# A quarter of the r projection for twelve head pairs, computed in fp32 inside the recurrence

## The chip, the cores and the metric

The kernel runs on one core of one Trainium2 chip. The metric is the device time of one execution in microseconds (us); the times of before are those of three runs, and the rows of the trace come from a fourth, profiled one. PE is the matrix engine (TensorE), PEld its weight loads, DVE the vector engine (VectorE), ACT ScalarE, POOL GpSimd, SP the engine that issues nearly all DMAs; "SPq" in a row is SP's queue.

## What is computed

One inference step of a two-layer decoder: an RWKV-7 layer and an RG-LRU layer, each followed by a causal ConvFFN, for a prompt of 256 rows and a group of 8 sample rows (T = 264 columns, model width 2048 = 16 tiles of 128). The change lies in the RWKV layer:

```python
xx = x_prev - x
xr, xw, xk = x + xx * mix[0], x + xx * mix[1], x + xx * mix[2]
...
r = xr @ w_r
k = xk @ w_k
v = xv @ w_v
...
def _wkv_step(S, inp):
    r_t, d_t, k_t, v_t, a_t, b_t = inp
    sa = jnp.einsum('bhvk,bhk->bhv', S, a_t)
    S = S * d_t[:, :, None, :] + sa[..., None] * b_t[:, :, None, :] + v_t[..., None] * k_t[:, :, None, :]
    y = jnp.einsum('bhvk,bhk->bhv', S, r_t)
    return S, y
```

r, k and v are 2048 wide, that is 16 pairs of heads of 64; the scan `_wkv_step` runs over time for every head. All values are float32.

## The kernel before

Values stand transposed: a tile has 128 channels in its partitions and 264 columns (256 prompt, 8 sample). `U0` first holds x, then the mixer's input h, and from the end of the projections on r.

**Projections** (loop over `PARTS` and `projs`, L820 to L858). The 16 input tiles are taken in five parts, the last being tiles 12 to 15; for each part the projections k, v and r follow each other, each in four groups `g` of four output tiles. A matmul of the projections is done in three passes (`mm_pieces`, L446): weights and inputs are split into a rounded high part (`wh`, `ah`) and the rest (`wl`, `al`) of type fp32r, and high x high, high x low and low x high are added in PSUM. Weights come as a stream `ws` of pieces (1024 columns, half of a raw tile of 1 MB), loaded by SP (L419) and split by ACT and DVE (L433, L434) two pieces ahead. Partial sums of parts 0 to 3 stay in `acck`, `accv`, `accr`; after the last part `last_k`, `last_v` send k and v to DRAM (`Kd`, `Vd`), and `last_r` (L800) writes `accr` + PSUM into `U0`. Ahead of the last r projection stands `lora()` (L803 to L816), which makes `lw` from three further mixes of h; its matmuls are plain fp32, with weights not split. With part 12 to 15, the r projection's four groups of two pieces are the last work of this stage.

**Recurrence** (`wkv_begin` to `wk.close()`). Every pair j of heads goes through jobs, written as generators: load, prep, diag, solve, levels, prepb, seq, out; beside them run the sample group (sprep, sixteen pieces `sample`, sgate, send) and 44 "pump" steps, which compute the modulation vectors for later layers from raw tiles of 1 MB (`wm`, L344; loads L1400). A step is what stands between two `yield`s. The order of all steps is a table written out, `ORDER`: a letter names the job, a number in front says how many steps, the number behind is the pair (`3p0`: three steps of prep for pair 0). Every engine then works through its instructions in that order. Prep starts with lora weights `lu` and the row `kj` of k from `Kd`; PE (L972, L974) and ACT make `sa`, DVE `kk`, the scan `cum`, products `b` and `AR` (which needs r, in `U0`); PE multiplies `b` x `AR` (L898); `ma` is copied out, goes through DRAM (`scr`, L1064) to `mb` (L1069) for the solve on DVE (pairs 0 and 1) or POOL, comes back as `xc` (L1096) to the levels, which make `E`, and the scan (seq) uses it, four chunks a pair. The copy `yh` (L1195) is the first step of out, after a pair's scan. Raw tiles in this stage have three buffers (`raw_tile`), shared by pumps and the sample group's weights (`lups`, L1246). After the last pair the out projection begins with pieces of `ws` again.

```python
        for h in range(2):
            SP.dma_start(raw[:, 1024 * h:1024 * h + 1024], I["wmr"][i][:, 1024 * h:1024 * h + 1024])
            yield
```

Of the kernel before, what the change touches and what calls it, by code (L numbers as in the profile page):

```python
# [38 lines left out]
p2 b1 p2 b0 2w1 b0 3p2 4p1 g0 b0 l3 l4 d1 p3 p2 l4 d0 b0 p2 2p3 2b1 w2 3b0 u0 w2 2p3 2p2 2p3 p4 p3 5p2 3p3 2p4
a0 d0 g0 d1 p4 2g0 b2 p2 u1 3b1 2s0 p3 h0 p3 2g0 d2 2l5 2p3 u2 d3 b1 p5 2w3 s0 d2 g0 s0 4g0 w4 g0 2s0 d3 2p4  # L40
2b1 2p3 b1 2p4 4b2 s2 p4 l6 p4 p3 2g0 2p4 w5 2p5 s2 4p5 3g0 4p4 b3 2p4 g0 2p5 u3 3p5 2g0 3b2 b3 p5 2b3 s0 p5
g0 p5 b3 2p5 v0 3p6 2v0 w4 2v0 u4 l6 v1 q0 g0 p6 s2 2g0 a0 l7 p4 v0 p5 w6 v1 p5 s2 3a0 2s2 l7 2p6 a0 p6 2q0
3p7 b2 2v1 w5 u5 2p7 b2 2p6 w6 u6 v0 p6 p7 2p6 2v1 2v0 2b3 2v0 4a0 b3 3h0 2b3 l8 b4 4p7 l8 h0 s2 p8 p7 s4 d5
2p8 h0 2q0 v1 d4 p8 q0 p9 v1 q0 l9 w7 s2 v2 3p7 4h0 2q0 3v1 q0 d4 3q0 l9 2q0 2p9 a1 p7 d5 2q0 p7 s6 p7 p9 6p6
2p7 2q0 a1 2q0 b5 3v2 2q0 d7 2o0 l10 w8 b4 p6 v3 b4 q1 p8 l11 2v2 2q1 w8 q1 v3 2s4 3p8 2v2 v3 a1 w7 s4 q1 2p8
v2 u7 o0 2s4 q1 v3 3q1 v2 q1 d6 2p8 q1 p9 w10 a0 v2 v3 o0 v3 a1 2w9 w10 2a1 2p9 3q1 s4 q1 3a1 2p8 l10 2q1 d6
d7 3o0 s6 q1 o0 a1 u8 u9 2p10 p9 p8 2o0 2p10 3a2 u10 2b4 2a2 b4 a1 3q1 s4 v4 v3 b4 2v3 3a2 2q1 v5 p9 3v4 2v3
2p8 3b5 2b4 2b5 p8 2p9 a2 p9 w12 2o0 v4 b5 b4 2w11 w12 b5 u11 u12 v4 s6 2b5 o0 2o1 l11 6q2 v4 q0 2w13 u13 o0
2v4 2a2 p8 s6 2v5 o1 3a3 2w15 2v4 w14 p9 v5 3q2 2p9 2q2 a3 2p9 a3 d8 p9 2s6 3q2 p10 p11 q2 w14 2o1 2p11 p10
2q2 p9 q2 2v5 2p10 w16 2a3 3q2 o1 s10 d8 q2 s6 2a3 p11 q2 o2 2o1 u14 u15 o1 o2 p10 w16 2p10 q3 p10 v5 3q3 o2  # L50
u16 2v5 a4 v5 p12 o1 v5 s6 v6 b6 2o2 q1 v6 d9 2q3 p11 a3 q3 2a4 b6 a3 p10 3q3 l12 v6 w17 a4 q2 2a4 v6 b6 q3 a4
2b6 3q3 w17 4p10 a4 o1 b6 q3 v6 2b6 p10 l12 3q3 v6 q3 p11 s8 q3 b6 2q3 o3 2a4 o3 a5 q3 a5 w18 p10 w18 b6 2p12
2o2 u17 b7 o2 l13 3q4 b7 p11 3p12 d9 2q4 w19 u18 b7 w19 d10 2o2 5p11 2w20 l13 a5 4q4 2v6 3v7 p12 v7 v6 a5 o2
q4 a4 2s8 p12 2p11 v6 o1 2q4 u19 v6 p12 2o1 o2 s8 2w21 d11 2q4 2p11 a6 3q4 2v7 2p11 w22 p11 q4 w22 3q4 p13 3a5
p13 2o2 p13 2q4 u20 2l14 2p13 u21 o3 p13 o3 2p12 o4 v7 2p12 o4 o3 q5 a5 o4 p14 2a5 2s8 v7 a6 2v7 2w23 q3 s8
2p12 4q5 p13 v7 p12 p14 p12 w24 3a6 o3 a6 2p14 a6 w24 3q5 o4 u22 u23 2q5 2o3 q5 2o3 s8 3o4 2q5 b8 3q5 v8 o3
2b7 2o4 b7 q5 o4 q5 v8 2p12 2b7 a6 q5 2v8 a5 2b8 q5 b8 a6 o3 q5 d10 q4 l15 2p13 3b8 2b7 2v8 2q5 u24 d11 s10
3b8 2w25 2o5 v8 q6 2w26 2s10 2q6 a6 2a7 v8 u25 v8 2q6 v9 2p14 p13 2v8 a7 3q6 2a7 o4 b9 2o3 q6 a7 2b9 a7 3q6
2w27 2o4 l15 u26 o4 p13 u27 s10 3o5 p15 2b9 3p13 w28 q6 w28 w29 2q6 s10 3p13 w29 a7 3q6 a6 b9 s10 q6 q5 q6 2b9
q6 p14 3v9 2q6 3p15 b9 2o5 w30 u28 2p13 b9 3o6 u29 q7 v9 b10 q7 2o5 w30 p14 o5 s14 v9 b10 2a7 b10 3p14 d12 3q7  # L60
3v9 o6 s12 u30 v9 a8 p14 p15 s10 2q7 v9 2q7 p15 o6 p14 p15 q7 2b10 2a8 w31 v10 w31 3q7 2p14 q7 d13 b10 2q7 v10
2a8 2q7 u31 2w32 q7 p14 2v10 b10 2q7 3a8 2p15 a7 q7 2o7 q7 a8 q8 p14 2v10 q6 u32 4q8 v10 2o5 v11 q8 v10 2o5
2v10 d12 d13 s12 2w33 q7 v10 q8 p15 a8 p15 2q8 b11 p15 5b11 q8 o6 a8 b11 2o7 3q8 3a9 q8 u33 3o6 2w34 q8 p14 o7
3q8 o6 w35 a9 o6 w35 p15 2q8 2p15 q8 s12 w36 2p15 s12 a9 o7 2s12 2q8 2o7 2o8 q9 s12 2o6 w36 d14 2q9 a10 2q9 o7
2q9 u34 a9 w37 o6 p15 u35 3q9 d15 2o7 v11 w37 s12 2a9 d14 d15 o8 o7 2a9 p14 2v11 4q9 w38 q9 2o8 a10 q9 u36 q9
a10 4q9 2v11 q9 w38 2o9 q8 q10 p15 2o7 o9 o8 o9 3q10 2o8 a9 2a10 v12 b10 q9 u37 a10 o9 q10 3o9 3o8 2b10 b11
2o9 v12 o9 b12 2q10 2b12 o9 2b11 v12 u38 3q10 s14 2a10 s14 v12 2b12 3q10 s14 q10 q9 v12 b13 2a10 2a11 b13 2q10
2b13 3b12 v12 b13 5q10 o8 w40 o8 o9 5a11 o9 o8 2b12 2q10 o10 a10 3b14 o10 b14 w40 b14 2b13 q11 2o10 2a11 o10
2v11 2q11 2a11 o10 2s14 a12 2v11 4o10 s14 2w39 2b13 v13 b13 v11 2q11 2b14 q10 2q11 s14 3v13 2v12 2q11 w43 2a12
q11 3a12 b14 2v13 3v12 q11 o10 a13 a12 b15 a12 3q11 u39 u40 2a12 3q11 2b14 2q11 2a13 2v13 3q11 o11 a12 a14 b15  # L70
2a13 o11 q12 q11 b15 v13 q11 v13 4q12 3a13 v13 q12 v15 v14 2b15 q12 3o11 2q12 o10 2v14 o11 q12 2a13 b15 o11
3q12 2b15 w42 a14 2q12 3o11 q12 a13 2v14 a15 4q12 o11 a14 q12 v14 b15 q12 b15 2o12 q13 o11 q12 2o10 4q13 2o12
o11 3a14 4o12 v15 4q13 o12 2v15 o11 2a14 o12 q13 o12 q12 2q13 2o12 3q13 2a14 o12 2q13 2v14 a15 4q13 2a15 v14
# [1723 lines left out]
```

## Time and profile before

| | us |
|---|---|
| median of 3 runs (2865.06 to 2867.12) | 2866.76 |
| the profiled execution | 2867.66 |
| its span, first to last instruction | 2865.9 |
| end of the last r projection, from the span's start | 398.0 |
| first matmul of the out projection | 728.06 |

The profiled execution is 0.9 us over the median. Projections take the first 398 us, the recurrence 330 us, and the other layers the rest. In the rows below a time is a start in us from the span's start and the number behind it a duration; `[... <-x]` is how long the engine had been idle and what ended that. "x4" are four instructions in a row: an fp32 matmul is two of them, a matmul of the split kind is one. PEclk is the share of full clock that was granted to PE: 1.00 is 2.4 GHz, 0.50 is 1.2 GHz, and what lies between is a mean of both.

### The profile page before, as it was taken

To read this page: it belongs to the slowest core of one execution; us is meant where nothing else is said; L and a number is where in the kernel's file an instruction comes from. 1 tells how busy PE (TensorE), PEld (TensorE's weight loads), DVE (VectorE), ACT (ScalarE), POOL (GpSimd) and SP (SyncE) were. 2 spreads that over 40 slices of the span, in tenths; PEclk is the share of its full clock that TensorE was granted. 3 is DMA by queue.
4 is the path that set the end of the run, shared out by engine and by line. 5 is a ranking of instruction groups with operands and counts; after the bars stand their busy time and mean duration, and the time that the engine had idled before them with its cause. 6 is when DMAs were issued, how large, how long until landed. Compare 5 with 4: busy or idle time off the path is not lost.

```text
span 2865.9 us, 61683 instructions
## 1 busy us (share of the span) xinstructions
...
## 2 busy tenths in 40 slices
...
GB/s 329 291 259 242 209 121 237 254 263 155 278 247 225 240 249 254 257 247 237 251 254 250 253 241 192 265 228 246 249 228 250 206 179 184 181 177 179 183 187 75
DMA packets 146134, 648.48 MB, mean 226 GB/s; under 512 B 41104, under 2 KB 60704, under 8 KB 77248
## 3 DMA queue, kind: packets, MB, share of 16 engines
...
## 4 chain that ended last, share of the span: by engine, by line
PE 83%; DVE 6%; ACT 3%; DMA 3%; issue 2%; POOL 1%; SPq 0%; DVEq 0%; POOLq 0%; ACTq 0%
PE bk L454 18%; PE bk L455 17%; PE bk L456 17%; PE sq L454 7%; PE sq L455 7%; PE sq L456 7%; PE wm L344 5%; DVE wl L434 1%; PE bk L898 1%; DMA raw<-in_wmr 1%; ACT wh L433 1%; DMA rawx<-in_wst 1%; DVE bt L548 1%; PE sq L812 1%; POOL xs L1087 1%
## 5 line engine op out<-in xcount | busy, mean ns | idle before, releaser
L434 DVE TENSOR_TENSOR wl<-raw,wh 128x1024 fp32r<-128x1024 f32 x448 | 552.3, 1235 | 498.6 <-ACT wh L433 489.5
L433 ACT CAST wh<-raw 128x1024 fp32r<-128x1024 f32 x448 | 468.6, 1048 | 643.6 <-PE bk L455 430.0
L454 PE MATMUL bk<-AH,wh 128*128 128x264 f32 x2352 | 670.6, 285 | 0.9 <-ACT wh L433 0.9
L456 PE MATMUL bk<-AH,wl 128*128 128x264 f32 x2352 | 669.1, 284 | 1.7 <-DVE wl L434 1.5
L455 PE MATMUL bk<-AL,wh 128*128 128x264 f32 x2352 | 668.7, 284 | 0.8 <-DVE AL L492 0.8
L434 DVE TENSOR_TENSOR wl<-rawx,wh 128x1024 fp32r<-128x1024 f32 x312 | 381.6, 1225 | 331.7 <-ACT wh L433 326.6
L433 ACT CAST wh<-rawx 128x1024 fp32r<-128x1024 f32 x312 | 326.5, 1048 | 457.8 <-PE bk L455 337.4
L454 PE MATMUL bk<-ah,wh 128*128 128x264 f32 x1822 | 524.8, 289 | 9.8 <-ACT ah L491 5.5
L456 PE MATMUL bk<-ah,wl 128*128 128x264 f32 x1822 | 520.9, 286 | 0.4 <-DVE wl L434 0.4
L455 PE MATMUL bk<-al,wh 128*128 128x264 f32 x1822 | 521.2, 286 | 0.0
L454 PEld LDWEIGHTS bk<-AH,wh 128*128 128x128 f32 x2352 | 443.3, 188 | 20.2 <-ACT cv L1537 8.4
L456 PEld LDWEIGHTS bk<-AH,wl 128*128 128x128 f32 x2352 | 441.7, 188 | 2.7 <-DVE wl L434 2.7
L455 PEld LDWEIGHTS bk<-AL,wh 128*128 128x128 f32 x2352 | 442.6, 188 | 1.0 <-DVE AL L492 1.0
L454 PEld LDWEIGHTS bk<-ah,wh 128*128 128x128 f32 x1822 | 344.1, 189 | 28.1 <-ACT wh L433 8.7
L456 PEld LDWEIGHTS bk<-ah,wl 128*128 128x128 f32 x1822 | 344.8, 189 | 1.5 <-DVE wl L434 0.8
L455 PEld LDWEIGHTS bk<-al,wh 128*128 128x128 f32 x1822 | 345.0, 189 | 0.7 <-DVE al L492 0.2
L454 PE MATMUL sq<-AH,wh 128*128 128x264 f32 x1040 | 296.7, 285 | 0.1
L455 PE MATMUL sq<-AL,wh 128*128 128x264 f32 x1040 | 295.6, 284 | 0.0
L456 PE MATMUL sq<-AH,wl 128*128 128x264 f32 x1040 | 295.4, 284 | 0.0
L1530 POOL COPY fgs<-gt 128x10 f32<-128x10 f32 x88 | 53.2, 632 | 1307.7 <-ACT gt L1524 1286.7
L454 PEld LDWEIGHTS sq<-AH,wh 128*128 128x128 f32 x1040 | 196.0, 188 | 9.6 <-ACT cv L1537 4.2
L455 PEld LDWEIGHTS sq<-AL,wh 128*128 128x128 f32 x1040 | 195.7, 188 | 0.0
(462 smaller groups left out, 4490.2 us busy)
## 6 DMA issues: line engine op xcount, KB each, us to landing
...
```

The lines of the kernel that those rows point to most:

```text
L344: PE.matmul(ps[32 * g:32 * g + 32, :cols], cs[:, k0 + kk, :], raw[:, (kk * 4 + g) * cols:(kk * 4 + g + 1) * cols], start=(k0 + kk == 0), s ...
L433: S.copy(wh, t)
L434: V.tensor_sub(wl, t, wh.bitcast(F32))
L454: PE.matmul(ps[:, :n], h[:, kk, sl], xh, start=first and kk == 0, stop=False)
L455: PE.matmul(ps[:, :n], h[:, kk, sl], xl, start=False, stop=False)
L456: PE.matmul(ps[:, :n], l[:, kk, sl], xh, start=False, stop=last and kk == 1)
L548: e.tensor_tensor(t, U1[:, j:j + n, :TP], r1[:, None, :TP].to_broadcast([128, n, TP]), op=mult)
L812: PE.matmul(pl[m][:, :T], pc[:, j % 2, m * 128:m * 128 + 128], xm, start=(j == 0), stop=(j == 15))
L898: PE.matmul(out[HH[(i + turn) % 2]], lhs[HH[i]], rhs[HH[i]], start=start, stop=stop, skip_group_check=True)
L1087: E.tensor_tensor(xs[:, s + 1:, :m], xs[:, s + 1:, :m], tv, op=add)
L1530: G.tensor_copy(gs[:, m], gt[:, TP:])
```

## The change

The last r projection (part 12 to 15) keeps group 0 only, so `last_r` runs for the tiles of pairs 0 to 3. For the other twelve pairs POOL copies `accr`, the sum of parts 0 to 3, into `U0`, after lora has read `U0` for the last time. The four mixes of tiles 12 to 15 for r are kept whole in a new tile `mr`. In the recurrence a new job `rest` (letter x) for i = 0, 1, 2 loads the raw tile of two pieces of w_r, multiplies in plain fp32 (four output tiles, four input tiles each, 264 columns: 16 matmuls), and DVE adds each result into `U0`. The stream `ws` ends six pieces earlier in the projections and is set to its old place after the recurrence. `ORDER` is new as a whole.

```diff
-p0 p1 2g0 2l0 2p0 l1 p1 p0 s0 l1 p0 g0 3p0 l2 4p0 p1 l3 2p0 2w0 5p1 2p0 4p1 p2 3p0 p2 2g0 p3 p2 l2 p2 3p1 3b0
...
+s0 g0 p0 l0 2p0 p1 3x0 2l1 l0 p1 g0 5p0 g0 p1 p0 3x0 5p1 p0 w0 p0 l2 2p1 x0 p0 3x0 3p0 2p1 2p0 p2 b0 2p2 2l3
...
+    mr = vres([128, 4, T], F32, "mr")
...
-    ws.limit = P1
+    ws.limit = P1 - 6
...
     def mix_of(j, m, xx):
-        t = a1p([128, T], F32, "mx", 4)
+        t = mr[:, j - 12] if m == 0 and j >= 12 else a1p([128, T], F32, "mx", 4)
...
                 lora()
+                with tc.manual_schedule(engines={mybir.EngineType.Pool}):
+                    G.tensor_copy(U0[:, 4:, 1:], accr[:, 4:])
...
-            for g in range(4):
+            for g in range(1 if b == 16 and w == 2 else 4):
...
+    def rest_of_r(i):
+
+        raw = raw_tile()
+        for h in range(2):
+            SP.dma_start(raw[:, 1024 * h:1024 * h + 1024], I["wst"][(P1 - 6) // 2 + i][:, 1024 * h:1024 * h + 1024])
+            yield
+        w = raw.rearrange("p (a k m) -> p a k m", a=2, k=2)
+        for m in range(4):
+            ps = bank()
+            for k in range(4):
+                PE.matmul(ps[:, :T], w[:, k // 2, k % 2, 128 * m:128 * m + 128], mr[:, k], start=(k == 0), stop=(k == 3))
+            yield
+            r = U0[:, 4 * i + 4 + m, 1:]
+            V.tensor_tensor(r, r, ps[:, :T], op=add)
+            yield
...
+    ws.i = ws.ns = P1
+    ws.nl = P1 // 2
```

Three places show what the table moves. First SP, from the load of `Fm` (the first of the recurrence) on; in brackets stand the semaphores that each load waits for, `DMAHW` being an earlier DMA. Before:

```order
L879 DMA Fm_4760<-in_cst 128x512 [waits DMAHW0_49,PE_49]
L882 DMA Z_4763<-in_cst 128x128 [waits DMAHW1_49]
L957 DMA lu_4776<-in_lup 128x256 [waits DMAHW2_49,DVE_49,PE_49]
L960 DMA kj_4778<-Kd_96 128x256 [waits DMAHW3_49]
L957 DMA lu_4788<-in_lup 128x256 [waits DMAHW4_49]
L960 DMA kj_4801<-Kd_96 128x256 [waits DMAHW5_49]
L1246 DMA raw_4806<-in_lups 128x2048 [waits DMAHW6_49]
```

After:

```order
L883 DMA Fm_4563<-in_cst 128x512 [waits DMAHW5_49,PE_49]
L886 DMA Z_4566<-in_cst 128x128 [waits DMAHW6_49]
L961 DMA lu_4581<-in_lup 128x256 [waits DMAHW7_49]
L1405 DMA raw_4593<-in_wst 128x1024 [waits DMAHW0_49,Activation_49]
L1405 DMA raw_4593<-in_wst 128x1024 [waits DMAHW1_49]
L961 DMA lu_4601<-in_lup 128x256 [waits DMAHW2_49]
L964 DMA kj_4603<-Kd_96 128x256 [waits DMAHW3_49,PE_49]
L964 DMA kj_4605<-Kd_96 128x256 [waits DMAHW4_49]
L1250 DMA raw_4622<-in_lups 128x2048 [waits DMAHW5_49]
```

`raw` from `in_wst` is new, a block's weights; `lu` of pair 0 waited for DVE and PE and now waits for an earlier DMA only, while the wait for PE has gone to the first `kj`.

Second, PE from the first instruction behind the projections: L972 and L974 (L976 and L978 after) are a pair's lora and norm, L898 (L902) is `b` x `AR`, L1251 (L1255) the sample group's weights, L1411 the new matmuls. Before:

```order
L972 MATMUL bk_4780<-lw_98,lu_4776 128x256 x2
L974 MATMUL bk_4783<-rn_99,e4_112 128x256
L972 MATMUL bk_4790<-lw_98,lu_4788 128x256 x2
L974 MATMUL bk_4793<-rn_99,e4_112 128x256
L898 MATMUL bk_4831<-AR_4820,b_4810 64x128 x8
L917 MATMUL bk_4855<-ident_107,b_4810 64x64 x8
L972 MATMUL bk_4879<-lw_98,lu_4813 128x256 x2
L974 MATMUL bk_4882<-rn_99,e4_112 128x256
L1251 MATMUL bk_4884<-raw_4806,l8_4773 32x512 x4
```

After:

```order
L976 MATMUL bk_4583<-lw_98,lu_4581 128x256 x2
L978 MATMUL bk_4586<-rn_100,e4_113 128x256
L1411 MATMUL bk_4596<-mr_99,raw_4593 128x264 x4
L976 MATMUL bk_4607<-lw_98,lu_4601 128x256 x2
L978 MATMUL bk_4610<-rn_100,e4_113 128x256
L1411 MATMUL bk_4631<-mr_99,raw_4593 128x264 x4
L1411 MATMUL bk_4663<-mr_99,raw_4593 128x264 x4
L1411 MATMUL bk_4670<-mr_99,raw_4593 128x264 x4
L902 MATMUL bk_4678<-AR_4649,b_4619 64x128 x8
L921 MATMUL bk_4691<-ident_108,b_4619 64x64 x8
L976 MATMUL bk_4705<-lw_98,lu_4654 128x256 x2
```

The first block's four fourths stand between the lora of pairs 0 and 1 and pair 0's `b` x `AR`.

Third, PE where the levels of pair 0 begin (`X1` and `P1`, L904, L908 after). Before, with a pump step (L344) and the first chunk of pair 0's scan (`Vb`, `KQ`):

```order
L904 MATMUL bk_5436<-X1_5424,ma_4829 32x32 x16
L904 MATMUL bk_5458<-P1_5456,XT_5453 32x32 x16
L344 MATMUL wm_5026<-raw_5205,cT_72 32x512 x4
L898 MATMUL bk_5485<-Vb_4967,KQ_4916 64x64 x2
L904 MATMUL bk_5522<-X1_5482,ma_4901 32x32 x16
L898 MATMUL yb_5484<-KQ_4916,Vb_4967 64x64 x2
L898 MATMUL sq_5576<-Vb_4967,KQ_4916 64x64 x2
L972 MATMUL bk_5584<-lw_98,lu_5513 128x256 x2
```

After:

```order
L908 MATMUL bk_5219<-X1_5122,ma_4676 32x32 x16
L976 MATMUL bk_5236<-lw_98,lu_5109 128x256 x2
L978 MATMUL bk_5239<-rn_100,e4_113 128x256
L1411 MATMUL bk_5250<-mr_99,raw_5111 128x264 x4
L1411 MATMUL bk_5258<-mr_99,raw_5111 128x264 x4
L1411 MATMUL bk_5264<-mr_99,raw_5111 128x264 x4
L976 MATMUL bk_5282<-lw_98,lu_5204 128x256 x2
L978 MATMUL bk_5285<-rn_100,e4_113 128x256
L908 MATMUL bk_5291<-P1_5246,XT_5244 32x32 x16
L1411 MATMUL bk_5320<-mr_99,raw_5111 128x264 x4
L1133 MATMUL bk_5333<-X2_5308,ma_4676 32x32 x8
```

The second block stands among the levels; the first chunk of pair 0's scan has moved ahead of them.

## Rows read from the trace of the kernel before

**Rows 1.** Busy time in stretches: from:to, length, then the engines, PEclk, DMA.
```profile
core 0: us, PE busy (x) PEld busy (x) DVE busy (x) ACT busy (x) POOL busy (x), PEclk, DMA share, GB/s
...
374.00:398.00 24.00, 23.98 (x195) 23.70 (x193) 10.72 (x19) 7.19 (x11) 0.14 (x2) 1.00 0.05 14
398.00:412.00 14.00, 8.91 (x51) 6.68 (x55) 6.87 (x19) 7.69 (x16) 3.26 (x7) 0.63 0.88 270
...
640.00:700.00 60.00, 57.10 (x1358) 42.07 (x1354) 47.36 (x102) 27.98 (x93) 27.75 (x51) 1.00 0.55 160
...
398.00:520.00 122.00, 100.15 (x1795) 68.59 (x1795) 87.07 (x210) 63.11 (x153) 60.86 (x155) 0.89 0.81 250
398.00:728.00 330.00, 286.89 (x5764) 198.23 (x5764) 230.25 (x539) 169.23 (x455) 152.31 (x351) 0.92 0.73 227
```

**Rows 2.** Timeline of DVE at the end of the projections: start, us, instruction.
```profile
380.48 0.43 DVE L800 TENSOR_TENSOR U<-accr,sq 128x264 f32<-128x264 f32 x1
...
398.02 0.43 DVE L800 TENSOR_TENSOR U<-accr,bk 128x264 f32<-128x264 f32 x1 [0.30 <-PE bk L456]
```

**Rows 3.** Timeline of PE inside lora.
```profile
347.02 1.05 PE L812 MATMUL sq<-mx,raw 128*128 128x264 f32 x4
347.91 1.05 PE L812 MATMUL bk<-mx,raw 128*128 128x264 f32 x4
```

**Rows 4.** Timeline of SP's queue where the recurrence's loads begin.
```profile
374.62 0.33 SPq L879 DMA_DIRECT2D Fm<-in_cst  x1
...
397.89 0.33 SPq L957 DMA_DIRECT2D lu<-in_lup  x1
398.26 0.42 SPq L960 DMA_DIRECT2D kj<-Kd  x1
...
399.69 0.43 SPq L1246 DMA_DIRECT2D raw<-in_lups  x1
```

**Rows 5.** Waits of SP's queue, 374 to 398 us: total, times, longest.
```profile
SPq L957 <- DVE wl L434: 13.1, 1, 13.1
SPq L957 <- PE bk L456: 9.5, 1, 9.5
```

**Rows 6.** Timeline of all engines, 400 to 430 us.
```profile
400.23 1.17 PE L972 MATMUL bk<-lw,lu 128*128 128x256 f32 x4 [2.25 <-DMA lu<-in_lup]
...
403.23 0.48 DVE L983 SCALAR_TENSOR_TENSOR kk<-kj,par,bk 128x256 f32<-128x256 f32 x1 [4.42 <-DMA kj<-Kd]
...
406.29 0.42 DVE L933 TENSOR_TENSOR b<-b,ip 128x256 f32<-128x256 f32 x1
...
406.76 1.97 PE L898 MATMUL bk<-AR,b 64*64 64x128 f32 x16 [0.82 <-DVE b L933]
...
413.72 0.42 DVE L940 COPY ma<-bk 128x256 f32<-128x256 f32 x1
...
427.14 0.17 DVE L1085 TENSOR_TENSOR xtmp<-mb,xs 64x15 f32<-64x15 f32 x1 [2.57 <-DMA mb<-scr]
```

**Rows 7.** The same view, 430 to 462 us: POOL and DVE side by side.
```profile
440.12 0.91 POOL L933 TENSOR_TENSOR kc<-k,ip 128x256 f32<-128x256 f32 x1
440.37 0.95 DVE L933 TENSOR_TENSOR b<-b,ip 128x256 f32<-128x256 f32 x1
440.98 0.49 POOL L1288 COPY c<-U 128x128 f32<-128x128 f32 x1
```

**Rows 8.** Waits of PE in the recurrence, 397 to 722 us: total, times, longest.
```profile
PE bk L1251 <- DMA raw<-in_lups: 5.6, 1, 5.6
...
PE wm L344 <- DMA raw<-in_wmr: 2.4, 2, 2.2
```

**Rows 9.** Timeline of ACT: the copies yh after the scans of pairs 0 and 1.
```profile
479.12 0.37 ACT L1195 CAST yh<-yb 128x256 fp32r<-128x256 f32 x1
...
510.36 0.37 ACT L1195 CAST yh<-yb 128x256 fp32r<-128x256 f32 x1 [1.92 <-PE bk L1053]
```

**Rows 10.** The instructions of one line: the last step of the sixteen sample pieces.
```profile
L1359 DVE TENSOR_REDUCE sy<-smt x16: 654/685/686, 467.1 to 703.7; 128x8 f32<-128x512 f32 x16
```

More of the change, by code (lines that the diff above doesn't have):

```diff
@@ L32 @@
 NFA, NFH, NFB, NFZ, NFM, NFE = 8, 7, 4, 6, 7, 4
-JOBS = dict(zip("lpdsvbqoagheuw", ("load", "prep", "diag", "solve", "levels", "prepb", "seq", "out", "sample",
-                                    "sprep", "sgate", "send", "pump", "pl")))
+JOBS = dict(zip("lpdsvbqoagheuwx", ("load", "prep", "diag", "solve", "levels", "prepb", "seq", "out", "sample",
+                                     "sprep", "sgate", "send", "pump", "pl", "rest")))
 ORDER = """
-p0 p1 2g0 2l0 2p0 l1 p1 p0 s0 l1 p0 g0 3p0 l2 4p0 p1 l3 2p0 2w0 5p1 2p0 4p1 p2 3p0 p2 2g0 p3 p2 l2 p2 3p1 3b0
@@ L39 @@
[L39 to L73, printed above, removed]
@@ L74 @@
-3q13 3o13 q14 2a15 v14 v15 2q14 v14 7q14 v15 6q14 2v15 3a15 4q14 a15 e0 o13 v15 2q14 o14 e0 2o14 o13 2v15 q14
-4q15 e0 4q15 w41 q15 e0 7q15 h0 e0 q15 2e0 5q15 w41 o13 q15 o14 o15 w42 u41 u42 w43 u43 o14 o15 o13 o14 2o13
-2o14 5o13 6o14 q15 q14 a15 a14
+s0 g0 p0 l0 2p0 p1 3x0 2l1 l0 p1 g0 5p0 g0 p1 p0 3x0 5p1 p0 w0 p0 l2 2p1 x0 p0 3x0 3p0 2p1 2p0 p2 b0 2p2 2l3
+l2 w0 p0 p3 p2 2g0 p0 2p2 3p1 4p2 b1 2p3 p1 2w1 3p1 l5 d0 d1 2p2 w3 2p3 2b0 p4 2p3 b1 p2 b1 2p3 p2 p3 2p2 p3
+d0 d1 p3 g0 p2 s0 p2 s0 b0 u0 u1 3b0 2p3 3b1 h0 2p3 b0 2p5 w3 p2 2s0 b1 s0 l4 p3 p4 p5 2p3 2b0 p4 l4 2p4 w2 l5
@@ new lines @@
+2p5 w2 u2 u3 g0 q0 g0 2p4 3g0 b1 s0 3p5 2b2 2q0 2b2 5p4 3p5 l6 x1 2b1 s0 v0 d2 l6 x1 b2 g0 b2 p5 2g0 p6 3p4
+2b2 p5 d2 g0 p5 d3 d5 2g0 2p4 l7 2p5 l7 p5 v0 2p6 2v0 p6 2x1 p7 3x1 2p4 x1 2p6 l8 p6 p7 d3 2p5 2v0 2s2 x1 2p7
+v1 2v0 v1 2s2 2w4 p6 p7 b3 p6 2w5 u4 u5 x1 p6 v1 p6 2v0 2v1 2b2 v0 3q0 d4 b3 v1 q0 2b3 2q0 p7 3b3 q0 2p8 2h0
+d4 2p7 p6 2h0 q0 p8 h0 3q0 l8 p8 2p6 b4 4s2 p6 3q0 3b3 p7 s4 p7 2v1 d5 2x2 p7 2l9 3q0 2v2 p7 2v1 p7 q0 h0 v1
+2v2 a0 q0 o0 2p6 3p7 w7 2o0 2p6 l11 v3 2p7 2q1 v2 d7 q1 v2 4p9 p8 o0 2h0 2s4 2v2 2q1 v2 2b4 b5 o0 2v2 2p8 v3
@@ new lines @@
+a1 3o0 l10 h0 p7 v3 2x2 p9 q0 x2 v3 s4 w6 2s4 4o0 p9 3x2 p8 2x2 w6 p8 2q1 2p8 b4 d6 4q1 b4 2g0 s4 2g0 2p9 3g0
+u6 w7 u7 v3 2q1 b4 2g0 3q1 s4 g0 v4 b4 2v4 l10 4v3 d6 d7 2w8 2s6 u8 v4 b4 v3 4q1 2g0 2a0 w9 q0 q1 a0 v3 a0 s6
+3b5 w11 3b5 b4 p8 3a0 b4 2a0 w9 p10 b5 o0 u9 b5 q1 v5 q1 b5 o0 2p8 2w10 2o1 w11 3p10 w12 s6 2o1 u10 u11 o1 p8
+3q2 s6 a0 p9 p8 d8 3a1 2q2 v5 p8 2p9 s6 q2 v5 p9 2q2 v4 v5 q2 2p8 v5 v4 a1 p10 q2 v5 a1 q2 a1 w12 w14 3p9 w14
+q2 p10 a1 q2 p9 l11 4q2 2p10 3p9 p10 a2 w13 3v4 w13 3q2 a1 d9 b6 2a1 b6 p11 3q2 v4 o1 b6 2o2 u12 s6 v4 o1 q3
@@ new lines @@
+p10 a2 d8 p11 2q3 a2 q3 b7 2o1 q1 u13 2a2 p11 o1 d9 2v5 o1 v5 p11 o2 2l12 p11 q3 u14 2v5 s8 4q3 2p10 3a2 b6 a2
+p12 s8 q2 b6 a2 2b6 q3 o2 a3 p11 3a3 p12 o2 3q3 s6 p11 2q3 p12 2w15 p11 a3 v6 2a3 p10 p12 b6 s8 a2 s8 2q3 6p10
+2q3 b6 2a3 2v6 4q3 b6 o1 2o3 q4 o2 a3 2o2 l13 u15 2b7 3q4 v6 w16 2o2 w16 q4 2v6 4p11 2o1 w18 q4 a3 q4 2v6 l13
+3a4 q4 s10 2q4 s8 u16 w18 p12 2v7 2v6 o2 d10 2v7 a4 l15 q4 2v7 2a4 v6 p12 3q4 a4 2o3 3q4 p13 2p11 a4 p11 a5 a4
+2w17 4q4 2w19 o3 p11 p12 q4 q3 b8 q4 p13 a4 2p12 2p11 a5 l14 p11 2o4 p12 v7 u17 2p12 u18 2p13 a4 3v7 2p13 v7
@@ new lines @@
+2q5 s8 p12 3q5 2p12 d11 q5 2a5 s8 3p12 2w20 a6 2q5 2p13 o3 p13 o3 2p14 q5 u19 u20 w21 l14 o2 a5 3o3 2o2 w22 a5
+p14 2q5 a5 s8 v8 o4 b8 q5 p14 3q5 2b8 a5 2q5 w21 2a5 2b7 4q5 b8 a6 b7 2o3 q5 p12 q4 q5 o4 v8 a6 o3 2b7 a6 2o4
+2v8 u21 a6 b7 o3 v8 a6 2p14 d10 o4 a6 o4 b8 d11 a6 b7 v8 2o4 2b8 2p13 w22 u22 3p14 2b8 2w23 l15 v8 2o5 p15 u23
+3v8 3s10 q6 v8 o5 p13 a5 2p13 4q6 p13 3b9 w25 2q6 3a6 2q6 3p13 2q6 v9 w25 2a7 3p15 v9 q6 p13 q6 b9 w24 2v9 w24
+q5 a8 b9 2q6 o4 2b9 2q6 p15 3a7 w26 2v9 2q6 2o5 u24 s10 p15 u25 d12 2s10 3o4 b9 2p15 2b9 p15 2q6 4a7 2q6 o6 v9
```

18 lines of the change are left out of this document (added).

## The prediction

> **What bounds the kernel now.** I read the trace by stage first [rows 1], since the change sits at one seam. From 374 to 398 us, the end of the projections, PE is busy 23.98 of 24 us at full clock, VectorE 10.7 and the DMA engines hardly at all (0.05): this stretch is as long as its matmuls. From 398 to 728 us, the recurrence, nothing is full: PE 287 of 330 us at a mean granted clock of 0.92, VectorE 230, DMA 0.73. The spare PE time is not spread evenly. In the first 122 us (398 to 520) PE idles 21.9 us, and its mean clock of 0.89 means that about 22% of that time, 27 us, runs at the lower level of 1.2 GHz, worth another 13 us of work. In 640 to 700 PE idles 2.9 us at a clock of 1.00. So work added early can cost nothing, and work added late costs its length. Then I read why the beginning is slow. The first loads of the recurrence stand on SP behind a wait for the last weight split and the last projection matmul [rows 5]; they are issued at 397.89 [rows 4], so PE starts pair 0 at 400.23, and pair 0's K row lets VectorE start at 403.23 and PE follow at 406.76 [rows 6]. By then the clock has fallen: 0.63 over 398 to 412 [rows 1].
>
> **What is removed.** Three of the four groups of the last r projection. The add that closes group 0 starts at 380.48, the one that closes group 3 at 398.02 [rows 2]: 17.54 us, all of it PE at full clock, so all of it on the path. Six weight splits and three loads of 1 MB go with it; they lay beside that PE time and give nothing more.
>
> **What is added.** 48 fp32 matmuls of 264 columns. The lora matmuls are the same form: two of them (four PE instructions) every 0.89 us [rows 3], so 0.445 us each, 21.4 us in all, in three blocks of 7.1 us. The twelve adds of VectorE are not new: they stood in the projection. On paper the sum is 21.4 - 17.5 = 3.9 us more PE work; the change pays only if the recurrence swallows the blocks. The first 122 us have 21.9 + 13 = 35 us to spare, and in the new order all three blocks stand ahead of the end of pair 1's scan, which before came at 510.36 [rows 9]. So they go where the room is. The two ends: below nothing if the blocks fill gaps and keep the clock up as well (I take 10 us below, under the 13 us that the low clock cost), and all of 21.4 us. I take 0, by the stretch of rows 1 that the blocks land in.
>
> **Block by block.** Let T be the end of the projections, 398.0 before and 380.5 (same clock) after. The new program's first load of lora weights for pair 0, and the raw tile of block 0, wait for neither the last split nor the last matmul (first pair of listings above): other tiles now lie where the last split weights lie. SP comes to them right behind the load of Fm, which went out at 374.62 [rows 4], so both should be there at T. PE then goes on without a gap: pair 0's lora (1.3 us), the first fourth of block 0 (1.8), pair 1's lora (1.3), the rest (5.3), done at about T + 10. Only the K rows still wait for the end: issued at T + 0.5, and before it took from 398.26 to 403.23 until kk could use one [rows 4, 6], so kk at about T + 5, as before (T + 5.2). Behind kk stand on VectorE two adds of block 0 (0.43 each) and pair 1's kk, scan and product, so pair 0's first products b x AR come at about T + 10.6, against T + 8.8 at 406.76 [rows 6]. That is 1.8 us late, but at full clock: the same sixteen instructions took 1.97 us then. Pair 1's should come as before. From there the new order is shorter: the copy ma of pair 1 ended at T + 16.2, but the solve, which needs its diagonal back from DRAM, began only at 427.14, T + 29 [rows 6]; now the loads mb stand right behind the stores scr on SP, with one raw load between, and I expect the solve at T + 24. The 5 us of lead are the cover for block 1, which stands in the levels of pair 0, where PE waits for small steps of the other engines. Block 2 stands within pair 1's scan, ahead of the sample group's transposes. If the lead isn't there, block 1 costs its 7.1 us.
>
> **The copy on POOL.** U takes over accr for twelve tiles, 3168 columns, as one instruction. The row of a POOL copy is 0.49 us for 128 columns, a POOL product of 256 columns 0.91 [rows 7], so 3.6 to 3.8 ns a column, 11.3 to 12.1 us (an estimate). It can start at about 372.5, when the last mix of the lora has read U, and ends about 384.5, T + 4; the first add that needs it stands at T + 6. So it adds nothing as long as it ends by then. VectorE could feel it in a second way: its product b took 0.95 us at 440.37 while POOL's kc ran until 441.03, and 0.42 at 406.29 with POOL quiet [rows 6, 7], so it seems to have waited for POOL. In the 12 us of the copy VectorE has only the adds of group 0, which read PSUM and one tile of SBUF; I take 0 here, and price a longer copy below, as (e). The Trainium skill, "SBUF — State Buffer", section "SBUF: two separate sides", has a rule that speaks against such a copy: a GpSimd instruction and a VectorE instruction with two SBUF inputs take one port pair for their whole length, and whichever comes later waits. By that rule, the trace agrees (0.95 against 0.42), and a copy of 12 us would leave the sum at 2849, one of 25 us would make it the 2857 of (e).
>
> **The sum.** The profiled run took 2867.66 us (span 2865.9), 0.9 over the median of 2866.76. 2867.7 - 17.5 + 0 = 2850.1; less 0.9 for the median, **2849 us**.
>
> **The rivals.** (a) *The lead is carried to the end*: pair 0 starts 5 us sooner, the low clock of 398 to 412 (0.63, some 5 us of work lost) does not occur, and both last: 10 us below, 2839. For it: the second half has little idle and so keeps a lead. Against it: the later pairs may be held by PE, which has the same work left. Chance 0.13. (b) *Blocks 1 and 2 on the path*: the lead is lost in the levels of pair 0 and both cost their 14.2 us: 2863.5. For it: PE takes its rows in order, and the levels are a chain through PE. Against: 21.9 us idle. Chance 0.11. (c) *VectorE becomes the bound*: the sample group waits for the last r, so its sixteen pieces, which began with the first reduce at 467.1 [rows 10], start some 30 us later against T, and two pieces (8 us of VectorE) and the adds (5 us) fall into the rest. VectorE is at 70% over the recurrence and reached 79% in 640 to 700 [rows 1]; if that is its most, 13.4 / 0.79 = 17 us: 2866. Chance 0.06. (d) *Slower*: blocks 1 and 2 wait for their weights. All raw tiles share a ring of three, so their loads queue behind pump tiles not yet used, and PE, in order, stands still. The nearest row is the sample weights, for which PE waited 5.6 us once; all 44 pump tiles together cost 2.4 us [rows 8]. Price: (5.6 + 7.1) x 2 = 25.4, so 2849.2 + 25.4 = 2874.6. It decides from 11.6 us for each block on the path, 23 in all. Chance 0.09. (e) *The POOL copy is twice my estimate*, 25 us: it ends at T + 17, VectorE stands at the first add of block 0 from T + 6 on, and pair 0's product comes some 8 us late even if the adds behind it close up: 2857. For it: no POOL row is as long, so the price is stretched from short ones. Chance 0.05. That the change does nothing isn't open: the 17.5 us are out of the PE rows.
>
> **How the numbers follow.** The forecast (between 2843 and 2857, the absorbed share a few us to either side) has 0.56. Within 0.2%, about what a measurement of this kernel can tell from no change, is 2861.0 to 2872.5. Faster: forecast, (a), (e) and a quarter of (b), 0.77. Same: the rest of (b), and (c), 0.14. Slower: (d), 0.09. Range: 2836 to 2865, which leaves out (c), (d), a rest of (b) and the far end of (a), 0.19.
>
> **What would show it.** Right: the last projection matmul near 380 us and pair 0's lora right behind it with no idle PE; the raw tile of block 0 issued at 375 to 377; the new matmuls 0.44 us apart, with a granted clock of 1.00 over the first 14 us after T; the first solve step near T + 24; pairs 0 and 1 done (the copies yh) at about T + 80 and T + 112, where 479.12 and 510.36 [rows 9] are T + 81 and T + 112; the recurrence 330 us long. Wrong: PE waiting for raw ahead of a new matmul (d), a clock of 0.5 there, a POOL copy over 13 us (e), VectorE over 79% with PE waiting for it (c), or pair 1 done later than T + 120 (b). The sum is most at risk in the recurrence's later part, which I did not price: its order is new throughout.

## The result and the profile after

The changed kernel takes 2850.89 us (median of 4, 2847.40 to 2855.22) against 2866.94 us for the kernel before (4 runs): a ratio of 0.9936, 95% interval 0.9924 to 0.9948. Measured again (e5) the ratio was 0.9930 (0.9918 to 0.9942). Forecast were 2849 us and a range of 2836 to 2865. The profiled execution took 2848.57 us with a span of 2846.8, that is 19.1 us less than the profiled one of before.

Where the time went is read from two points. The last add of the projections, which answers to [rows 2]; timeline of DVE of the changed kernel (start, us, instruction):

```profile
377.14 0.43 DVE L802 TENSOR_TENSOR U<-accr,bk 128x264 f32<-128x264 f32 x1 [5.83 <-PE bk L457]
...
379.33 0.43 DVE L802 TENSOR_TENSOR U<-accr,sq 128x264 f32<-128x264 f32 x1 [0.30 <-PE sq L457]
```

And the first matmul of the out projection, behind the recurrence; timeline of PE:

```profile
710.04 0.59 PE L455 MATMUL bk<-ah,wh 128*128 128x264 f32 x1 [3.67 <-ACT wh L434]
```

The projections end at 379.33 instead of 398.02, 18.7 us sooner. The recurrence takes 710.04 - 379.33 = 330.7 us; it took 330.0. What follows takes 2136.8 us; it took 2137.8. So the sum is 18.7 - 0.7 + 1.0 = 19.0, and the 21.4 us of new matmuls have left 0.7 us in the stage in which they stand. (The end of the projections lies between 377.1 and 380.9 in the twelve profiles with the shortened projection, and at 402.1 in e2, which keeps it whole, so of the 18.7 some two us either way may be chance. The 0.7 is within the scatter too: e12, no slower than the changed kernel, has a recurrence of 335.7 us.) Why they cost nothing is seen in the stretches behind the projections, to be held against [rows 1] (columns as there):

```profile
379.33:393.33 14.00, 11.92 (x79) 9.50 (x77) 8.12 (x23) 7.32 (x14) 1.89 (x5) 1.00 0.91 305
...
379.33:501.33 122.00, 106.99 (x1813) 76.96 (x1813) 78.77 (x206) 61.70 (x148) 60.33 (x153) 0.98 0.80 246
379.33:710.04 330.71, 291.60 (x5861) 206.82 (x5859) 234.51 (x552) 170.05 (x455) 157.52 (x350) 0.96 0.76 233
```

The first 14 us have a granted clock of 1.00 (0.63 before), the first 122 us 0.98 (0.89), and PE idles 15.0 us there (21.9). Busy time by clock is 106.99 x 0.98 = 104.9 against 89.1 us: 15.7 us more work in the same 122 us, some 7 of it out of idle time, the rest out of the clock. The start itself, PE and SP:

```profile
379.13 1.03 PE L976 MATMUL bk<-lw,lu 128*128 128x256 f32 x4
379.81 0.47 PE L978 MATMUL bk<-rn,e 128*128 128x256 f32 x1
380.16 1.13 PE L1411 MATMUL bk<-mr,raw 128*128 128x264 f32 x4
382.13 1.16 PE L1411 MATMUL bk<-mr,raw 128*128 128x264 f32 x4 [0.84 <-DMA raw<-in_wst]
...
385.50 5.61 PE L1411 MATMUL bk<-mr,raw 128*128 128x264 f32 x24 [1.23 <-DVE kk L987]
391.04 1.09 PE L902 MATMUL bk<-AR,b 64*64 64x128 f32 x16
```

```profile
374.34 0.42 SPq L961 DMA_DIRECT2D lu<-in_lup  x1
374.86 0.85 SPq L1405 DMA_DIRECT2D raw<-in_wst  x2
375.76 0.43 SPq L961 DMA_DIRECT2D lu<-in_lup  x1
379.20 0.80 SPq L964 DMA_DIRECT2D kj<-Kd  x2
```

Pair 0's lora follows the last projection matmul at once, since its weights were asked for at 374.34 [rows 4: 397.89 of 398.0]. The first product b x AR comes 391.04 - 379.33 = 11.7 us behind the end.

### The profile page after: what moved, and what is told of

Same layout as the page of the kernel before. It is cut to its first block, busy times and chain, and to the rows that moved or that the text cites. A ratio compares the mean times of both kernels' runs of the same rounds, so it can differ in the third digit from the quotient of the medians.

```text
span 2846.8 us, 61582 instructions
## 1 busy us (share of the span) xinstructions
PE 2740.7 (96%) x25820; PEld 2526.2 (89%) x25820; DVE 1753.7 (62%) x2824; ACT 1358.7 (48%) x2187; POOL 524.4 (18%) x1045
## 4 chain that ended last, share of the span: by engine, by line
PE 86%; DVE 7%; ACT 2%; DMA 2%; issue 1%; POOL 1%; SPq 0%; DVEq 0%; ACTq 0%; POOLq 0%
PE bk L455 18%; PE bk L456 18%; PE bk L457 18%; PE sq L455 7%; PE sq L456 7%; PE sq L457 7%; PE wm L345 5%; DVE wl L435 1%; PE bk L902 1%; ACT wh L434 1%; DVE bt L549 1%; PE bk L908 1%; PE bk L814 0%; PE sq L814 0%; DVE U L550 0%
## 5 line engine op out<-in xcount | busy, mean ns | idle before, releaser
L455 PE MATMUL bk<-ah,wh 128*128 128x264 f32 x1786 | 514.6, 289 | 9.2 <-ACT ah L492 5.5
L457 PE MATMUL bk<-ah,wl 128*128 128x264 f32 x1786 | 510.6, 286 | 0.5 <-DVE wl L435 0.5
L456 PE MATMUL bk<-al,wh 128*128 128x264 f32 x1786 | 510.6, 286 | 0.0
L455 PEld LDWEIGHTS bk<-ah,wh 128*128 128x128 f32 x1786 | 337.6, 189 | 27.6 <-ACT wh L434 8.1
L457 PEld LDWEIGHTS bk<-ah,wl 128*128 128x128 f32 x1786 | 338.1, 189 | 1.4 <-DVE wl L435 0.8
L456 PEld LDWEIGHTS bk<-al,wh 128*128 128x128 f32 x1786 | 338.4, 189 | 0.6 <-DVE al L493 0.2
```

Source lines behind the costliest of these rows:

```text
L455: PE.matmul(ps[:, :n], h[:, kk, sl], xh, start=first and kk == 0, stop=False)
L456: PE.matmul(ps[:, :n], h[:, kk, sl], xl, start=False, stop=False)
L457: PE.matmul(ps[:, :n], l[:, kk, sl], xh, start=False, stop=last and kk == 1)
```

## The experiments

Each was timed against the kernel before on its own chip. "Over" is the difference to the changed kernel, taken as the ratio less 0.9933 (the middle of its two measurements), times 2870 us; the intervals make that uncertain by some 3 to 5 us. yh is the copy after pair 0's scan, counted from the last add of the projections, and the recurrence goes from that add to the first matmul of the out projection, both from the one profile of each kernel.

| kernel | ratio, 95% interval | over, us | pair 0's yh | recurrence |
|---|---|---|---|---|
| before | 1 | 19 | 81.1 | 330.0 |
| changed | 0.9936 (0.9924 to 0.9948) | 0 | 75.2 | 330.7 |
| changed, again (e5) | 0.9930 (0.9918 to 0.9942) | 0 | 75.1 | 331.1 |
| e1 no blocks | 0.9941 (0.9925 to 0.9957) | 2 | 77.4 | 335.3 |
| e2 order alone | 1.0001 (0.9989 to 1.0014) | 20 | 75.1 | 329.5 |
| e3 old order | 0.9989 (0.9977 to 1.0002) | 16 | 95.6 | 352.6 |
| e10 old order, no loads | 0.9973 (0.9961 to 0.9984) | 11 | 87.5 | 341.0 |
| e7 old order, blocks later | 1.0024 (1.0014 to 1.0035) | 26 | 94.7 | 366.8 |
| e6 all early | 0.9999 (0.9989 to 1.0010) | 19 | 97.1 | 351.4 |
| e9 all early, no loads | 0.9970 (0.9958 to 0.9982) | 11 | 86.9 | 340.6 |
| e8 block 0 later | 0.9965 (0.9953 to 0.9978) | 9 | 82.5 | 341.8 |
| e11 late loads | 0.9953 (0.9940 to 0.9966) | 6 | 80.1 | 338.7 |
| e4 K row first | 0.9950 (0.9935 to 0.9964) | 5 | 77.2 | 339.0 |
| e12 pair 0 first | 0.9933 (0.9920 to 0.9945) | 0 | 75.3 | 335.7 |

### What the blocks cost where they stand, and what the order is worth alone

```diff
-            ps = bank()
-            for k in range(4):
-                PE.matmul(ps[:, :T], w[:, k // 2, k % 2, 128 * m:128 * m + 128], mr[:, k], ...)
             yield
-            r = U0[:, 4 * i + 4 + m, 1:]
-            V.tensor_tensor(r, r, ps[:, :T], op=add)
             yield
```

> The changed kernel without the 48 fp32 matmuls of the three blocks and without their twelve adds (their loads stay), so a quarter of r is missing for twelve pairs. It prices the blocks in their place. Theory A, the forecast's: they fill idle PE time and half clock, 0 to 7 us of 21.4 lie on the path, so 2844 to 2851 us against 2850.9 for the changed kernel. Theory B: they cost their full 21.4 us, and the new order of the other steps pays for them: 2829.5 us. In the trace, by A: with the blocks out the clock over the first 14 us behind the projections falls to 0.6 to 0.8, and the first matmul of the out projection comes 324 to 331 us behind the projections; by B 309.

0.9941: leaving 21.4 us of PE work out saves nothing. The profile shows what then stands in their place, by the stretches behind its projections' end at 380.85, and by PE's waits in the first 122 us (total, times, longest):

```profile
380.85:394.85 14.00, 3.35 (x12) 2.26 (x12) 5.47 (x15) 6.93 (x13) 1.88 (x5) 0.62 0.86 263
...
380.85:502.85 122.00, 95.56 (x1797) 66.48 (x1796) 76.54 (x198) 62.19 (x152) 59.03 (x153) 0.86 0.79 245
```

```profile
PE bk L976 <- DMA lu<-in_lup: 9.8, 3, 4.5
PE bk L902 <- DVE b L937: 6.5, 1, 6.5
```

In the first 14 us PE works 3.35 us, at a clock of 0.62. Over the 122 us it idles 26.4 us at 0.86, where the changed kernel idles 15.0 at 0.98: busy time by clock is 82.2 against 104.9 us, a difference of 22.7, which is the blocks. Theory A holds in the time and the clock, though the recurrence, 335.3 us, is 4 us over its range; theory B is off by 20 us.

The blocks' loads stayed in e1, and part of its room may be theirs: pair 1's lora weights were asked for right behind block 0's raw tile, and PE waited for them; timeline of PE:

```profile
385.97 2.05 PE L976 MATMUL bk<-lw,lu 128*128 128x256 f32 x4 [4.18 <-DMA lu<-in_lup]
```

The next kernel has neither the blocks nor their loads.

Then the other half, the kernel before with the new table less its x steps:

```diff
-ORDER = (the table of before)
+ORDER = (the new table without 10x0, 10x1, 10x2)
```

> The kernel before (r whole in the projections) with the new order of all other steps, the blocks' steps struck out. Theory A: the new order is worth little by itself, 2860 to 2868 us against 2866.9. Theory B: it is worth what the blocks cost, some 21 us: 2845.5 us. The recurrence, 330.0 us before, would be 323 to 331 us by A and 309 by B.

1.0001: the new order by itself is worth nothing. Its pairs end where those of the changed kernel end (yh of pair 0 at 75.1 and 75.2 us, recurrence 329.5 and 330.7), with the blocks or without. Its room is about that of e1: behind its projections' end at 402.10 PE idles 26.1 us of 122, at a clock of 0.85.

```profile
402.10:524.10 122.00, 95.94 (x1781) 67.32 (x1779) 75.71 (x199) 62.53 (x153) 60.37 (x156) 0.85 0.74 223
```

So the blocks stand in waits that this order has anyway, without their loads too.

### Whether the place matters

e3 is the changed kernel with the table of before; block 0 stands as in the new one, blocks 1 and 2 between the preparation steps of pairs 2 to 4.

```diff
-s0 g0 p0 l0 2p0 p1 3x0 2l1 l0 p1 g0 5p0 ...
+p0 p1 2g0 2l0 2p0 3x0 l1 p1 p0 s0 l1 p0 g0 3p0 l2 p0 3x0 2p0 x0 p0 3x0 p1 l3 2p0 2w0 2x1 ... w2 2x2 ...
+(8x1 spread from d0 to u0, 8x2 from d2 to the 18th g0)
```

> The changed kernel with the order of before for all old steps; block 0 stands where the new order has it, blocks 1 and 2 are spread between the preparation steps of pairs 2 to 4, ahead of the sample group's transposes, which this order has 43 us behind the projections. Theory A: room in the first 45 us before was 11.6 us of idle PE and some 8 us worth of half clock, so 0 to 5 us are left on the path: 2850 to 2856 us. Theory B: the old order has no gain to pay with, 2866.9 - 18.0 + 21.4 = 2870 us.

It lost 16 of the 19 us: nearer to theory B's number, but not for its reason, since e2 shows no gain of the order that could pay. Pair 0's solve starts late, on a load; timeline of DVE, and the waits of SP in 378 to 425 us:

```profile
421.22 0.17 DVE L1088 TENSOR_TENSOR xtmp<-mb,xs 64x15 f32<-64x15 f32 x1 [5.44 <-DMA mb<-scr]
```

```profile
SPq L1419 <- PE wm L344: 5.1, 1, 5.1
SPq L1404 <- PE bk L1410: 4.1, 2, 3.0
```

The solve starts 421.22 - 377.70 = 43.5 us behind the projections, against 29.1 before [rows 6]. SP stood for raw tiles that a pump (L344) or a block (L1410) still read, with the loads mb behind them. e10 takes that away: the blocks' matmuls multiply by a slice of `mr` and load nothing.

```diff
-        raw = raw_tile()
         for h in range(2):
-            SP.dma_start(raw[:, 1024 * h:1024 * h + 1024], ...)
             yield
-                PE.matmul(ps[:, :T], w[:, k // 2, k % 2, 128 * m:128 * m + 128], mr[:, k], ...)
+                PE.matmul(ps[:, :T], mr[:, k, :128], mr[:, k], ...)
```

> The same for the kernel with the order of before and the blocks inserted (15 us over the changed kernel): matmuls as they are, no loads for them. In its profile the loads mb of pair 0 were issued 34 us behind the projections (22.5 before), behind raw loads that waited for buffers. Theory Q: with the loads gone 0 to 5 us over the changed kernel. Theory P: PE's time ahead of pair 0's steps is the cost, 10 to 15 us over it.

The solve came at 33.3 us, and of the 16 us 11 remained, theory P's size. So some 5 us went with the loads; the two ratios alone don't tell that from chance, but the solve came 10.2 us sooner behind the projections. The other 11 I put down to PE time in wrong places. That is argued: no run has the order of before with the shortened projection and no blocks. e7 put blocks 1 and 2 in this table where the new one has them, and the sample group behind them.

```diff
-... w4 2v0 u4 ... v1 q0 ... w6 u6 ... q1 ...
+... w4 2x1 2v0 u4 ... v1 x1 q0 ... w6 2x2 u6 ... q1 x2 ...
+(8x1 from the first v1 to the sixth s2, 8x2 in q1; g0 from its 19th step and all a but the first behind them)
```

> As the old-order kernel, but blocks 1 and 2 stand where the new order has them (among the levels of pair 0, and within pair 1's scan), and the sample group's transposes and pieces are held back until behind block 2. Theory P (the place of blocks 1 and 2 cost the 15 us): within 4 us of the changed kernel. Theory O (the old order of the other steps leaves no holes to fill): 10 us or more over it, as the old-order kernel was.

26 us, worse than e3, where theory P allowed 4; PE waited 8.4 us there for the sample weights, which share the ring. The holding back of the sample group is part of that, so e7 doesn't price the places alone. Whether some other placing would fit the order of before is open; these two by hand did not.

e6 asks the same of the new order: all three blocks at the start.

```diff
-... p1 3x0 2l1 l0 p1 g0 5p0 g0 p1 p0 3x0 5p1 p0 w0 p0 l2 2p1 x0 p0 3x0 3p0 ...
+... p1 2x0 2x1 2x2 x0 2l1 l0 p1 g0 5p0 g0 p1 p0 3x0 5p1 p0 w0 p0 l2 2p1 x0 p0 3x0 8x1 8x2 3p0 ...
```

> The changed kernel with blocks 1 and 2 moved up behind block 0, so that all three stand ahead of pair 0's first b x AR. Theory P (the room is in holes between the steps of the pairs, so the blocks have to stand in them): pair 0 comes 14.2 us later, little of it is given back, 8 to 14 us over the changed kernel. Theory A in its plain form (35 us to spare in the first 122, anywhere): 0 to 4 us over it, with pair 0's yh later but pair 2's not.

19 us, all of the gain. Timeline of PE, and SP's waits in 377 to 440 us:

```profile
388.18 2.07 PE L975 MATMUL bk<-lw,lu 128*128 128x256 f32 x4 [7.17 <-DMA lu<-in_lup]
389.69 0.77 PE L977 MATMUL bk<-rn,e 128*128 128x256 f32 x1
390.26 20.83 PE L1410 MATMUL bk<-mr,raw 128*128 128x264 f32 x88
411.03 1.09 PE L901 MATMUL bk<-AR,b 64*64 64x128 f32 x16
```

```profile
SPq L1249 <- PE bk L1410: 17.0, 1, 17.0
SPq L1419 <- PE bk L1410: 9.9, 2, 6.7
```

With three blocks in the ring of three, SP stood 27 us for their buffers, and PE waited 7.2 us for pair 1's lora weights, asked for behind them. The product b x AR came at 33.9 us.

> The kernel with all three blocks at the start, but without the blocks' loads: their 48 matmuls multiply the kept mixes by a slice of the same tile, so r is wrong for twelve pairs while PE does the same work, and neither SP nor the ring of three raw tiles sees the blocks. That kernel with loads was 20 us over the changed one, and SP stood 27 us behind raw tiles that block matmuls still read. Theory Q (the ring and SP's order cost the most): 5 us or less over the changed kernel. Theory P (14.2 us of PE work on the path of pair 0): 12 to 15 us over it.

Without the blocks' loads 11 us remained of 19; b x AR came at 23.3 us, yh 11.7 us later than in the changed kernel. So 8 us went with the blocks' loads, and 11 us stayed with their matmuls and adds: theory P's size, a little under it.

### What carries to the end

e8 moved three of the four fourths of block 0 behind pair 0's b x AR.

```diff
-... p1 p0 3x0 5p1 p0 w0 p0 l2 2p1 x0 p0 3x0 3p0 2p1 2p0 ...
+... p1 p0 5p1 p0 w0 p0 l2 2p1 2p0 2x0 2p0 2x0 2p1 2p0 2x0 ... p0 x0 ...
```

> The changed kernel with three of the four fourths of block 0 moved behind pair 0's b x AR, where PE waits for the copies ma and for the solve. That product should come at 8 to 9 us behind the projections instead of 11.7, and the solve at 23 instead of 26. If the first pair's time is carried: 3 us under the changed kernel. If, as the profiles so far show, a lead of pair 0 is gone by pair 2: the same within 2 us.

Neither: it is 9 us slower, and the product came at 11.9 us all the same. Timeline of PE:

```profile
384.06 0.47 PE L977 MATMUL bk<-rn,e 128*128 128x256 f32 x1
391.00 1.97 PE L901 MATMUL bk<-AR,b 64*64 64x128 f32 x16 [6.48 <-DVE b L936]
392.90 4.86 PE L1410 MATMUL bk<-mr,raw 128*128 128x264 f32 x16
```

PE waits 6.48 us for VectorE's `b`, at half clock by then (the product takes 1.97 us, not 1.09). VectorE had itself waited 4.84 us for the K row and 1.39 us for pair 1's `sa` (timeline of DVE), so `b` was done 11.9 us behind the end, with the block ahead of the product or not. PE's wait for it is what the 5.6 us of block 0 fill in the changed kernel; moved out of it they cost at least about their length: pair 0's yh is 7.3 us later, and the end 9.

e4 meant to take the early start away, by the K row's load ahead of pair 0's lora weights.

> The changed kernel, but pair 0's load of its lora weights and the loads of block 0 stand on SP behind the load of its K row, which waits for the last projection matmul; all else as it is. PE should then start 2 to 3 us after the projections end, and block 0 wait for its raw tile until 5 to 6 us after, so that pair 0's first b x AR comes at 14 to 15 us instead of 11.7. Theory A: pair 0's lead was used up by pair 2 in any case, 0 to 2 us: 2851 to 2853. Theory C: the early start is what pays for the first block, 4 to 8 us: 2855 to 2859.

The edit did something else: its tiles lie otherwise, the K row no longer waits for the last matmul, and pair 0's weights still went out early (374.45). Only pair 1's were late; PE waited 1.1 us for them, and the product came at 14.3 us. The 5 us it cost say nothing on the early start. e11 does, with a store that has to wait for the last add:

```diff
+        if j == 0:
+            dz = drp([128, 8], F32, "dz")
+            SP.dma_start(dz, U0[:, 3, 1:9])
         lu = d["lu"] = wk([128, 2, 128], F32, "lu", 2)
```

> The changed kernel with one small store of r's tile 3 (8 columns, to a DRAM tile that nothing reads) on SP ahead of pair 0's lora weights. It waits for the last add of the projections, so all loads of the recurrence are issued behind the end of the projections, as they were before. PE should start pair 0 some 2.5 us after the end, and pair 0's b x AR come 3 to 4 us later than in the changed kernel. If pair 0's time is carried, as the kernel with block 0 moved later suggests: 3 to 6 us over the changed kernel. If it is absorbed: 0 to 1.

```profile
381.59 2.05 PE L979 MATMUL bk<-lw,lu 128*128 128x256 f32 x4 [3.13 <-DMA lu<-in_lup]
...
395.78 1.09 PE L902 MATMUL bk<-AR,b 64*64 64x128 f32 x16 [1.14 <-DVE b L937]
```

PE idles 3.13 us (timeline of PE), the product comes at 17.3 us instead of 11.7 (5.6 us later, where 3 to 4 were expected), yh 4.9 us later, and the kernel is 6 us slower (3 to 6 were expected if carried). The store moved the K rows as well: they were asked for at 381.28, 2.8 us behind the end, instead of 379.20, 0.1 us ahead of it. So the 6 us are the price of both together. e2 has early loads too (399.04 of 402.1) and is no faster than before; I read that as the early loads paying for block 0, which no run shows by itself.

e12 went for a gain: VectorE's last steps ahead of b x AR in front of pair 1's scan, and the product ahead of the last fourth of block 0.

```diff
-... 3x0 5p1 p0 w0 p0 l2 2p1 x0 p0 3x0 3p0 2p1 ...
+... 3x0 2p1 p0 w0 p0 l2 p0 3p1 x0 2p1 x0 p0 x0 p0 x0 p0 2p1 ...
```

> The changed kernel with the last three VectorE steps ahead of pair 0's b x AR (AR twice, b) moved in front of pair 1's scan and product, and that product in front of the last fourth of block 0. VectorE had stood 1.4 us for pair 1's sa with pair 0's P ready. The product should come at 9 to 10 us behind the projections instead of 12. If a gain of pair 0 is carried as a loss is: 2 to 3 us under the changed kernel. If pair 1, whose steps now come later, takes over: the same, or up to 5 us over it.

The same, 0.9933. The product came at 10.4 us, but the solve at 26.3, as in the changed kernel (26.0): timeline of DVE

```profile
406.28 0.17 DVE L1089 TENSOR_TENSOR xtmp<-mb,xs 64x15 f32<-64x15 f32 x1 [1.08 <-DMA mb<-scr]
```

The solve waits for mb's way through DRAM, and the stores `scr` of both pairs stand together on SP (four from 395.53 on, 15.6 us behind the end; 14.8 in the changed kernel). So no version here beats the changed kernel.

> The changed kernel itself, as the measure for the three others on the same chip: 0.993 to 0.995 of the kernel before, by every theory. Its profile also shows how far the stage of the recurrence (330.7 us in its first profile) varies between executions; I expect 329 to 336 us, since the profiles of the first four runs differ by such amounts where the same work stands in the same order.

The ratio came as expected and the recurrence at its lower end, 331.1 us.

## Why the prediction was right, point by point

*What is removed*: right. Forecast 17.5 us, all on the path, found 18.7, within the scatter of that point (379.33 against 398.02).

*What is added, at nothing*: right as a sum, and shown by e1 and e2. In a row of 24 PE instructions twelve new matmuls took 5.61 us, 0.47 each; forecast was 0.445. The reading that the idle time and the low clock of the first 122 us are the room was right in size (11.4 us less idle than in e1, and the rest clock). But the step "they go where the room is" was too loose: it took any place in the stretch for good. e6 (19 us) and e8 (9 us) show that other places in it cost about as much as the block is long (9 us for the 5.6 moved in e8, 11 without loads for the 14.2 moved in e9). With the idle time of [rows 1] alone I would have taken e6 for as good as the changed kernel. That the blocks' places were the right ones I had not shown; the terms for it, rivals (b) and (d), had 0.20 between them, and that they fitted was in part luck.

*The early start*: right. The raw tile of block 0 was asked for at 374.86, PE had no gap at the end, the clock was 1.00 over 14 us, K's row let kk start at 5.6 us (forecast 5). Forecast for b x AR was 10.6, found 11.7: PE waited 0.84 us for the second half of the raw tile and 1.23 for kk, which reads one of the four PSUM banks that the matmuls take in turn. The value of this start, which the prediction did not give apart, is some 6 us together with that of the K rows (e11).

*The solve at 24 us*: found 26.0. *Pair 0 and 1 at 80 and 112*: found 75.2 and 108.3, so the lead was larger than forecast by 4 to 5 us. It was not the cover for block 1, as the prediction had it: e2, without the block, has pair 0 at 75.1, so block 1 took nothing from the lead up to there. *The recurrence 330 us long*: 330.7.

*Rival (a), the lead carried to the end*: it did not come, although pair 0 was 5.9 us early. By pair 2 it was gone (126.7 us; 127.1 before). Timeline of ACT, yh of pairs 0 and 2, of the changed kernel and then of e2:

```profile
454.48 0.37 ACT L1199 CAST yh<-yb 128x256 fp32r<-128x256 f32 x1 [0.37 <-PE bk L902]
...
506.05 0.37 ACT L1199 CAST yh<-yb 128x256 fp32r<-128x256 f32 x1 [0.58 <-PE sq L902]
```

```profile
477.21 0.37 ACT L1195 CAST yh<-yb 128x256 fp32r<-128x256 f32 x1 [0.37 <-POOL xtmp L1085]
...
528.66 0.37 ACT L1195 CAST yh<-yb 128x256 fp32r<-128x256 f32 x1 [1.74 <-PE sq L898]
```

But the reason given against it, that PE holds the later pairs, is not what the runs show. Within the new order what pair 0 loses is carried: yh later by 2.0, 4.9, 7.3, 11.7 and 21.9 us in e4, e11, e8, e9 and e6, the kernel slower by 5, 6, 9, 11 and 19. And e2, with no blocks, has the same lead at pair 0 and the same pair 2 (75.1 and 126.6 us). So the lead of the new order over the old at pair 0 is given back between pairs 0 and 2 by its own order, not by the blocks. Which of its steps do that I have not tried.

*Rival (b)*, blocks 1 and 2 on the path: excluded by e1 and e2. *Rival (d)*, the ring of raw tiles: in the changed kernel PE waited 1.3 us in all for the blocks' weights (two waits), so it didn't occur; its mechanism is real: the loads cost 8 us in e6 and, less surely, 5 us in e3, more through SP's order than through a wait of the blocks themselves (2.5 us of PE in e3). *Rival (c)*, VectorE: it works 234.5 us of 330.7, 71%, and the recurrence is no longer for it, so no; but its price was taken from a highest share of 79%, and a stretch of the changed kernel has 35.01 of 41 us, 85% (columns as in [rows 1]).

```profile
524.33:565.33 41.00, 35.94 (x778) 24.68 (x777) 35.01 (x75) 28.46 (x67) 22.32 (x44) 1.00 0.81 240
```

*The POOL copy*: the worst-sized term. Estimated at 11.3 to 12.1 us, it took 2.83; timeline of POOL:

```profile
371.43 2.83 POOL L834 COPY U<-accr 128x3168 f32<-128x3168 f32 x1 [3.69 <-issue]
```

I had scaled a copy of 128 columns and a product of 256 (0.49 and 0.91 us [rows 7]) by their columns. A copy of 8 columns shows that nearly all of such a copy's time doesn't grow with the columns (though one of 4 columns, `pc` at 388.31, took only 0.19 us); groups of POOL of the changed kernel, 330 to 375 us (count, then busy and mean ns):

```profile
L778 POOL COPY V<-sp 128x8 f32<-128x8 f32 x12 | 5.5, 459 | 12.5 <-DVE sp L777 12.0
```

The copy ended at 374.26, ahead of the end of the projections, so (e) fell, and VectorE, which did nothing from 371.31 to 377.14, could not feel it. The Trainium skill, "GPSIMD Engine Reference", section "Elementwise — side-by-side cycle accounting", has 1.03 cycles of 1.2 GHz per element for a body of few operations: 3168 columns would be 2.72 us by it (an estimate), and the trace agrees (2.83 us). That a VectorE product takes longer beside a POOL product is seen again here: AR at 397.60 took 0.95 us beside the kc of 397.36 (0.91 us), and 0.41 at 389.29 without one.
